# Spare times of an RWKV stage's small products, set place by place

## The chip, the cores and the metric

The kernel runs on one core of a Trainium2 chip. The metric is the time of one execution on the device in microseconds. Below, PE is the engine of the matrix products (TensorE), DVE is VectorE, ACT is ScalarE, POOL is GpSimd, and SP is the engine that issues most transfers (SyncE).

## The reference

One layer of a hybrid decoder is computed for 1024 prompt tokens and 8 x 8 sampled tokens, 1088 columns in all, in float32. Cut to what matters:

```python
h = rms_norm(x, norm_mix) * (1 + sc) + sh            # sc, sh, gt from c
P = h @ w_in                                          # 1024 -> 4352 columns
pr, pp, pg = split(P)                                 # RWKV, pooling, gates
# RWKV-7, 8 heads of 64:
def step(S, inp):
    sa = einsum("bhvk,bhk->bhv", S, -kk_t)
    S = S * w_t + sa * (kk_t * a_t) + v_t * k_t       # outer products
    return S, einsum("bhvk,bhk->bhv", S, r_t)
y = group_norm(y) + bonus;  o_r = y * (sigmoid(xg) @ g2)
o_p = causal means over windows 2, 4, 8, 16, minus the token, @ pool_w
merged = sig(g_r) * (o_r @ w_br_rwkv) + sig(g_p) * (o_p @ w_br_pool)
x = x + gt * (merged @ w_out)
x = x + gt2 * (square(relu(adaLN(x) @ w_ff1)) @ w_ff2)
y = rms_norm(x)
```

## The kernel before

All rows lie with features on the 128 partitions and tokens along the free axis. A float32 product with a weight is made of three products in a faster format, from a high and a low half of each operand (`whi`, `wlo` for weights; `hx` tiles for the rows). The 1088 columns are taken in three chunks of 364, 362 and 362, one PSUM bank each (`mm`, four banks). A job of such big products accumulates over eight blocks of weights for each chunk and is then emptied to SBUF by ACT (into `px`), or, in the eight last jobs of the stage (`op_job`), by DVE.

The first part of the kernel, up to about 702 us of the profile, is the stage in question. PE's stream of big products (`w_in`, the gates, then `op_job`) is the background, and the RWKV-7 recurrence runs beside it as a set of small products in the banks `w` (two) and `wc` (two). Four pairs of heads are worked one after the other, `f` = 0 to 3, and called head f below. The steps of each:

- `front(f)`: loads k and others from scratch in DRAM (`d_x`) into `wt` buffers (there are five), squares k on ACT, takes the norm of kk by `strips` (four small products, a square root on ACT, a reciprocal on DVE) and `fan` (a store to DRAM and two loads that spread it), and makes two tanh products (`wa` with `w2a2`).
- `scores` with `unit`: masked products of 64 tokens with each other.
- `inverse` on DVE and `level` on PE: the inverse of a triangular block, by products of 32x32 (`n16` with `xd`, `nd` with `zd`, `ao` with `x32`, `pt` with `z`).
- `affine`: the generators `first(u)` (z with `at`, emptied by ACT and DVE into `at` and `uv`) and `second(u)` (`ab` with `at`), for the two halves u of the tokens.
- `chain`: the recurrence over chunks of 64 tokens, S.
- `bonus(f)` and `post(f - 1)`: the bonus, the group norm (`sums`, or for the last head `piece` on each chunk), the output gate (`gate`), and a store of the result to `d_or`. For f = 3 post's rows stay in SBUF.

`pools` does the pooling branch's four products of three chunks each, tile `plw`.

The order of PE's instructions is written out by the program as it runs a planner: `Pace.run` keeps a time `t` that each product moves on by an estimated duration. It takes the next background product unless one of the generators (`chains`, `heads`, `pools`, `or_rows`) is due. A generator yields a `Need`: operands, banks, `wait`, `spare` and `slack`. It is due when

```python
def at(self):
    return max([self.k.clocks.ready(*self.aps) + self.spare] + [self.k.clocks.free(b, self.k.pb[b], self.banks.count(b)) + self.slack for b in set(self.banks)])
```

is at most `t`. Here `ready` is the planner's estimate of when the operands are there, and `spare` the nanoseconds that are added to it, 300 if nothing is given. So a larger spare puts a small product behind more big products in PE's order; it is not a wait on the chip. With `wait=0` a due product goes at once; otherwise it may be held back up to that many ns for a place where PE's mode changes anyway. When the background has nothing to give, `t` is moved on to the next due time, and the spare changes no order.

Once PE's order stands, `Ledger.schedule` plans the DVE instructions and the SP transfers against it with estimated durations, and `Ledger.fix` ties both engines to that order. ACT and POOL get theirs from the framework's own estimate of a time line. ACT and DVE take their instructions one after the other. A product of PE waits on the chip until its operands are there and its bank is empty.

Of the kernel before, what the change touches and what calls it, by code (L numbers as in the profile page):

```python
# [450 lines left out]
class Room:  # L451


    wait = 0
# [91 lines left out]
class K:  # L546
# [563 lines left out]
    def pools(self):  # L1110

        nc = self.nc
        self.pl = {}
        for g in range(4):
            plw = self.pxp.tile([P, P], F32, tag="plw", bufs=1, name=self.nm("plw"))
            nc.sync.dma_start(plw, self.io["pool_w"][:, g * 128:(g + 1) * 128])
            yield lambda: ("pool", g) in self.done
            z, zs, hi, lo = self.pl[g]
            for c0, n in CH:
                m = min(n, NPR - c0)  # L1120
                yield self.need(z[:, c0:c0 + m], plw, zs, wait=0, spare=6000)
                ps = self.ps("w")
                self.mm(ps[:, :m], plw, z[:, c0:c0 + m], start=True, stop=True)
                if m < n:
                    self.mm(ps[:, m:n], plw, zs, start=True, stop=True)
                sc = self.par("pool_scale", g)
                nc.scalar.activation(hi[:, c0:c0 + n], ps[:, :n], AF.Copy, scale=sc)
                nc.vector.scalar_tensor_tensor(lo[:, c0:c0 + n], ps[:, :n], sc, hi[:, c0:c0 + n].bitcast(F32), op0=ALU.mult, op1=ALU.subtract)
            nc.sync.dma_start(self.d_op[0][g], hi.bitcast(F32))
            nc.sync.dma_start(self.d_op[1][g], lo.bitcast(F32))  # L1130
            self.done.add(("op", g))


    def front(self, f):

        nc, io = self.nc, self.io
        fs = slice(f * 128, (f + 1) * 128)
        X = lambda b: lambda: ("X", b) in self.done
        w2a2 = self.sm.tile([P, P], F32, tag="sw", bufs=2, name=self.nm("sw"))
        nc.sync.dma_start(w2a2, io["w2a2"][:, fs])  # L1140
        yield X(12)
        wa = self.wt()
        nc.sync.dma_start(wa, self.d_x[12])
        yield X(4 + f)
        k, kk = self.wt(), self.wt()
        nc.sync.dma_start(k, self.d_x[4 + f])
        for c0, n in FH:
            nc.scalar.activation(kk[:, c0:c0 + n], k[:, c0:c0 + n], AF.Square, scale=self.par("k_k", f))
        yield self.need(kk, wait=0)
        self.strips(kk, 1.0, 1)  # L1150
        self.fan(kk, self.d_n[f])
        t1, tha = self.wt(), self.wt()
        for c0, n in FP:
            yield self.need(wa, w2a2, banks=("w", "w"))
            ps = self.ps("w")
            self.mm(ps[:, :n], w2a2[0:64, :], wa[0:64, c0:c0 + n], start=True, stop=True)
            nc.scalar.activation(t1[:, c0:c0 + n], ps[:, :n], AF.Tanh, bias=self.hp[:, f:f + 1], scale=0.5)
            ps = self.ps("w")
            self.mm(ps[:, :n], w2a2[64:128, :], wa[64:128, c0:c0 + n], start=True, stop=True)
            nc.scalar.activation(tha[:, c0:c0 + n], ps[:, :n], AF.Tanh, bias=self.hp[:, 4 + f:5 + f], scale=0.5)  # L1160
        yield self.need(kk, banks=(), wait=0)
        yield X(f)
        r = self.wt(wa)
        nc.sync.dma_start(r, self.d_x[f])
        e = self.row(self.p1, "e", 1, w=1112)
        ev = e[:, :1040].rearrange("p (c j) -> p c j", j=65)
        es = e[:, 1040:1112].rearrange("p (c j) -> p c j", j=9)
        nc.gpsimd.memset(ev[:, :, 0], 1.0)
        nc.gpsimd.memset(es[:, :, 0], 1.0)
        end = self.sm.tile([P, 24], F32, tag="end", bufs=2, name=self.nm("end"))  # L1170
        bk = self.p1.tile([P, NC, 2, 64], F32, tag="bk", bufs=1, name=self.nm("bk"))
        if f:
            yield lambda: ("c", f - 1, 0) in self.done
        for c0, n in FH:
            s, cs = slice(c0, c0 + n), slice(c0 // 64, (c0 + n) // 64)
            t, a, x = t1[:, s], tha[:, s], k[:, s]
            yield self.room()
            nc.vector.tensor_scalar(t, t, 1.0, None, op0=ALU.add)
            nc.vector.tensor_tensor_scan(t, self.kscan[:, :n], t, 0.0, ALU.mult, ALU.add)
            m = min(n, NPR - c0)  # L1180
            nc.scalar.activation(ev[:, c0 // 64:(c0 + m) // 64, 1:65], cut(t1[:, c0:c0 + m]), AF.Exp, scale=-HC)
            if m < n:
                nc.scalar.activation(es[:, :, 1:9], cut8(t1[:, NPR:NT]), AF.Exp, scale=-HC)
            nc.scalar.activation(t, t, AF.Exp, scale=HC)

            yield self.room()
            nc.vector.scalar_tensor_tensor(kk[:, s], x, self.par("k_k", f), kk[:, s], op0=ALU.mult, op1=ALU.mult)
            g = bk[:, cs, 0, :]
            nc.vector.tensor_scalar(g, cut(a), self.hp[:, 8 + f:9 + f], self.hp[:, 12 + f:13 + f], op0=ALU.mult, op1=ALU.add)
            yield self.room()  # L1190
            nc.vector.tensor_tensor(cut(x), cut(x), g, op=ALU.mult)
            nc.vector.scalar_tensor_tensor(a, a, 1.0, kk[:, s], op0=ALU.add, op1=ALU.mult)
            for h, hs in enumerate(HB):
                yield self.room()
                nc.vector.tensor_tensor(bk[hs, cs, h, :], cut(x[hs]), cut(t[hs]), op=ALU.mult)
                nc.vector.scalar_tensor_tensor(bk[hs, cs, 1 - h, :], cut(a[hs]), 0.5, cut(t[hs]), op0=ALU.mult, op1=ALU.mult)
            if c0 == 0:
                yield self.room()
                self.cur = dict(bk=bk, end=end, kk=kk, r=r, ev=ev, es=es, z=self.z, qs={})
                self.ra(self.cur, 0)  # L1200
        nc.gpsimd.tensor_copy(end[:, 0:16], ev[:, :, 64])
        nc.gpsimd.tensor_copy(end[:, 16:24], es[:, :, 8])
        yield X(8 + f)
        yield self.room()
        nc.vector.scalar_tensor_tensor(k, r, self.par("r_k", f), k, op0=ALU.mult, op1=ALU.mult)
        q = [self.wt(x, F32R) for x in (t1, tha)]
        self.halves(k, *q)
        v = self.wt(k)
        nc.sync.dma_start(v, self.d_x[8 + f])
        self.cur.update(q=q, v=v)  # L1210
# [163 lines left out]
    def level(self, d):  # L1374

        nc = self.nc
        ao, zd, xd, n16, z = d["ao"], d["zd"], d["xd"], d["n16"], self.z
# [7 lines left out]
                self.mm(at(ps, g, c), n16[g, c, :], xd[g, c, :], **tp(g))  # L1385
        nd = cut32(self.hv())
        nc.vector.tensor_tensor(nd, cut32(ps), self.kc("i32").unsqueeze(1).to_broadcast([P, 16, 32]), op=ALU.add)
        yield self.need(nd, zd)
        ps = self.ps("w")
        for c in range(16):  # L1390
            for g in G:
# [9 lines left out]
        for c in range(16):  # L1401
            for os in HB:
                lo = slice(os.start, os.start + 32)
# [17 lines left out]
    def affine(self, f, d):  # L1421


        nc, z = self.nc, d["z"]
# [40 lines left out]
        yield self.need(z, A[0], banks=("w", "w"))  # L1465
        beside(first(0))
        if f:
            yield self.need(z, *A, B[0], banks=("w", "w", "wc", "wc"))
            beside(first(1, 0.55), second(0, "wc", 0.55))
        else:  # L1470
            yield self.need(A[0], B[0], banks=("w", "w"))
            beside(second(0))
        self.done.add(("s", f, 0))
        if not f:
            yield self.need(z, A[1], banks=("w", "w"))
            beside(first(1))
        yield self.need(A[1], B[1], banks=("w", "w"))
        beside(second(1))
# [102 lines left out]
    def post(self, f):  # L1581
# [10 lines left out]
        def gate(*over):  # L1592
# [3 lines left out]
            nc.sync.dma_start(sg, self.d_x[13])  # L1596
            nc.sync.dma_start(bv, self.d_bv[f])
            for c0, n in CH:
                yield self.need(g2, sg[:, c0:c0 + n], wait=0)
                ps = self.ps("w")  # L1600
                self.mm(ps[:, :n], g2, sg[:, c0:c0 + n], start=True, stop=True)
                nc.scalar.activation(sg[:, c0:c0 + n], ps[:, :n], AF.Copy)
# [7 lines left out]

        def piece(c0, n):
            s = slice(c0, c0 + n)
            yield self.need(y[:, s], wait=0)
            ps = self.ps("w")
            self.mm(ps[:, :n], self.kc("bones"), y[:, s], start=True, stop=True)
            nc.vector.scalar_tensor_tensor(y[:, s], ps[:, :n], -1.0 / 64, y[:, s], op0=ALU.mult, op1=ALU.add)
            nc.scalar.activation(sq[:, s], y[:, s], AF.Square)
            yield self.need(sq[:, s], wait=0)
            ps = self.ps("w")
            self.mm(ps[:, :n], self.kc("bones"), sq[:, s], start=True, stop=True)  # L1620
            self.rinv(ps, n, sq[:, s], 1.0 / 64, 2)
# [17 lines left out]
        else:  # L1639
# [2 lines left out]
                self.halves(y[:, c0:c0 + n], hi[:, c0:c0 + n], lo[:, c0:c0 + n])  # L1642
            for c0, n in CH:
                s = slice(c0, c0 + n)
                yield self.need(hi[:, s], lo[:, s], wait=0)
                nc.vector.scalar_tensor_tensor(y[:, s], self.sums(hi[:, s], lo[:, s]), -1.0 / 64, y[:, s], op0=ALU.mult, op1=ALU.add)
                nc.scalar.activation(sq[:, s], y[:, s], AF.Square)
            yield self.need(sq, wait=0)
            self.strips(sq, 1.0 / 64, 2)
            self.fan(sq, self.d_n[4 + f])  # L1650
            yield self.need(sq, banks=(), wait=0)
            nc.vector.tensor_tensor(y, y, sq, op=ALU.mult)
            nc.scalar.activation(y, y, AF.Identity, bias=self.par("ln_b", f), scale=self.par("ln_w", f))
            yield self.need(y[:, 0:1], banks=(), wait=0)
            bv, sg = yield from gate(sq, hi)
            nc.vector.tensor_tensor(y, y, bv, op=ALU.add)
            nc.vector.tensor_tensor(y, y, sg, op=ALU.mult)
# [867 lines left out]
```

## Time and profile before

| what | value |
|---|---|
| median of 3 runs | 1579.59 us (1578.9 to 1580.49) |
| the profiled execution | 1579.88 us |
| its span, first to last instruction | 1577.5 us |
| stage of this change | about 54 to 702 us of the span |
| PE busy in the stage | 627.52 of 648.00 us |
| mean granted clock of PE, whole span | 0.991 |

Busy time is not time at full speed: the clock that the profile lists as granted to PE falls to one half in a few short stretches, and PE counts as busy in them. Of a wait the profile names the engine and the tile of the instruction that came last before it ended; "issue" means that it shows nothing that was waited for. Most engine instructions go through helpers, so that the line is L583 (products) or L402 (the rest), and the tiles tell them apart: `w<-wt,bones` and `w<-wt,kct` with 128x36x columns are group norm sums, `w<-wt,kct` with 128x272 are strips, `w<-ab,at` is `second`, `w<-at,z` is `first`, `w<-px,plw` is the pooling product.

### The profile page before, as it was taken

The numbers are of one execution on the slowest core, as the hardware profiler recorded it, in microseconds if no ns is written. First come the engines' busy times: TensorE is split into PE (matmuls) and PEld (weight loads), VectorE is DVE, ScalarE is ACT, GpSimd is POOL, SyncE is SP. The second block draws the span as 40 slices with busy tenths as digits, with TensorE's granted clock in tenths as the row PEclk, the third lists the DMA queues.
The fourth block names the chain that finished last, engine by engine and source line by source line (L and its number), as shares of the span: only waits on it lengthen the run. The fifth ranks groups of instructions, "written<-read, shape, count | busy, mean of one in ns | idle before, by whom it ended". The sixth has DMA issues, their size and how long they took to land.

```text
span 1577.5 us, 34072 instructions
## 1 busy us (share of the span) xinstructions
PE 1529.9 (97%) x13836; PEld 1428.5 (91%) x13836; DVE 1064.3 (67%) x1883; ACT 642.3 (41%) x1254; POOL 143.8 (9%) x231
## 2 busy tenths in 40 slices
PE   6999999999999998999999999999999999999997
PEld 2989788988998898889999999999999999999997
DVE  4476657948693856364545797899667796666776
ACT  5554353454335433331323572222334344334652
POOL 2100100000000000013501310000000050000000
PEclk9999999999999999999999999999999999999999
DMA  9242523345334424846874565665446996664754
GB/s 368 84 137 95 193 78 101 115 137 158 104 114 164 114 92 141 325 159 226 310 281 172 190 205 171 223 232 181 146 144 227 399 347 202 208 215 144 232 174 148
DMA packets 140412, 294.00 MB, mean 186 GB/s; under 512 B 37256, under 2 KB 44992, under 8 KB 140256
## 3 DMA queue, kind: packets, MB, share of 16 engines
q1 hardware_dynamic: 133872, 270.71, 50.2%
q10 hardware_dynamic: 4320, 14.00, 2.6%
q0 software_dynamic: 2064, 7.13, 1.4%
q8 instruction: 108, 1.77, 0.5%
q14 instruction: 48, 0.39, 0.1%
HBM read 214.44 MB, written 77.34 MB: 185 GB/s over the span
## 4 chain that ended last, share of the span: by engine, by line
PE 68%; DVE 6%; DMA 5%; ACT 2%; issue 1%; POOL 0%; SPq 0%; DVEq 0%; ACTq 0%; POOLq 0%
PE mm L583 46%; PE wc L583 11%; PE w L583 10%; DMA hid<-in_w_ff 2%; DVE hx L402 1%; DVE wlo L402 1%; DMA wt<-d_x 1%; DVE hv L402 1%; DMA t<-d_th 1%; DVE wt L402 1%; DMA hid<-in_w_ada_mlp 1%; DMA mg<-in_w_ff 1%; DVE mg L402 0%; ACT wt L402 0%; DMA wt<-d_n 0%
## 5 line engine op out<-in xcount | busy, mean ns | idle before, releaser
L583 PE MATMUL mm<-hx,whi 128*128 128x362 f32 (+2 forms) x2944 | 689.6, 322 | 8.5 <-ACT px L402 4.6
L583 PEld LDWEIGHTS mm<-hx,whi 128*128 128x128 f32 x2944 | 496.3, 189 | 31.6 <-issue 9.0
L583 PE MATMUL mm<-hx,wlo 128*128 128x362 f32 (+2 forms) x1472 | 462.5, 315 | 0.4 <-DVE wlo L402 0.4
L583 PEld LDWEIGHTS mm<-hx,wlo 128*128 128x128 f32 x1472 | 278.8, 190 | 1.4 <-issue 0.8
L583 PE MATMUL mm<-mg,whi 128*128 128x272 f32 (+2 forms) x1312 | 248.8, 288 | 2.2 <-ACT t L402 1.2
L583 PEld LDWEIGHTS mm<-mg,whi 128*128 128x128 f32 x1312 | 205.3, 188 | 7.2 <-issue 2.5
L583 PE MATMUL mm<-mg,wlo 128*128 128x272 f32 (+2 forms) x656 | 188.5, 287 | 0.0
L583 PE MATMUL wc<-hx,whi 128*128 128x272 f32 x896 | 170.4, 287 | 0.0
L402 ACT ACTIVATE whi<-hid 128x512 fp32r<-128x512 f32 x128 | 80.5, 630 | 150.5 <-PE mm L583 58.4
L583 PEld LDWEIGHTS wc<-hx,whi 128*128 128x128 f32 x896 | 140.3, 188 | 0.0
L583 PE MATMUL wc<-hx,wlo 128*128 128x272 f32 x448 | 128.8, 287 | 0.7 <-DVE wlo L402 0.7
L583 PEld LDWEIGHTS mm<-mg,wlo 128*128 128x128 f32 x656 | 123.5, 188 | 0.0
L402 DVE TENSOR_TENSOR wlo<-hid,whi 128x512 fp32r<-128x512 f32 x128 | 87.8, 688 | 44.6 <-ACT whi L402 43.5
L402 DVE TENSOR_TENSOR wlo<-wraw,whi 128x512 fp32r<-128x512 f32 x84 | 59.8, 713 | 64.9 <-ACT whi L402 63.4
L402 ACT ACTIVATE whi<-wraw 128x512 fp32r<-128x512 f32 x100 | 62.6, 628 | 99.0 <-PE mm L583 53.9
L583 PE MATMUL w<-hx,whi 128*128 128x272 f32 (+1 forms) x480 | 97.2, 296 | 0.0
L402 POOL TENSOR_TENSOR hx<-hx,rs 128x64 f32<-128x64 f32 x24 | 37.1, 1546 | 567.6 <-ACT hx L402 357.8
L583 PEld LDWEIGHTS wc<-hx,wlo 128*128 128x128 f32 x448 | 84.2, 188 | 0.9 <-DVE wlo L402 0.9
L583 PEld LDWEIGHTS w<-hx,whi 128*128 128x128 f32 x480 | 77.1, 188 | 0.8 <-issue 0.8
L583 PEld LDWEIGHTS mm<-mg,hx 128*128 128x128 f32 x576 | 72.8, 188 | 5.0 <-issue 5.0
L583 PE MATMUL mm<-mg,hx 128*128 128x272 f32 (+2 forms) x576 | 74.7, 289 | 0.0
L583 PE MATMUL w<-hx,wlo 128*128 128x272 f32 (+1 forms) x240 | 70.5, 295 | 0.2 <-DVE wlo L402 0.2
(292 smaller groups left out, 2209.5 us busy)
## 6 DMA issues: line engine op xcount, KB each, us to landing
t<-d_t SPq DMA_DIRECT2D x56, 544.0 KB, 4.5
hid<-in_w_ff SPq DMA_DIRECT2D x110, 256.0 KB, 4.0
d_t<-hx SPq DMA_DIRECT2D x102, 272.0 KB, 2.2
hid<-in_w_ff SPq DMA_DIRECT2D x42, 512.0 KB, 3.9
wraw<-in_w_in SPq DMA_DIRECT2D x68, 256.0 KB, 2.8
mg<-in_w_ff SPq DMA_DIRECT2D x58, 256.0 KB, 5.3
hid<-in_w_ada_mlp SPq DMA_DIRECT2D x24, 512.0 KB, 5.3
d_th<-px SPq DMA_DIRECT2D x22, 544.0 KB, 3.3
```

The costliest lines, as they stand in the source:

```text
L402: r = f(*a, **kw)
L583: r = self.nc.tensor.matmul(out, lhsT, rhs, **kw)
```

## The change

Only numbers of `spare` change: in `pools` 6000 becomes 6700; the places in `front`, `affine`, `gate`, `piece`, the sums, the strips and the row `y` of `post` go from the default 300 to 600, 1000 or 1500; the second need of `level` goes from 300 to 100. The estimated durations, the instructions and the transfers are the same.

```diff
 pools:   - yield self.need(z[:, c0:c0 + m], plw, zs, wait=0, spare=6000)
          + yield self.need(z[:, c0:c0 + m], plw, zs, wait=0, spare=6700)
 front:   - yield self.need(kk, wait=0)
          + yield self.need(kk, wait=0, spare=600)
          - yield self.need(wa, w2a2, banks=("w", "w"))
          + yield self.need(wa, w2a2, banks=("w", "w"), spare=600)
 level:   - yield self.need(nd, zd)
          + yield self.need(nd, zd, spare=100)
 affine, f > 0:
          - yield self.need(z, *A, B[0], banks=("w", "w", "wc", "wc"))
          + yield self.need(z, *A, B[0], banks=("w", "w", "wc", "wc"), spare=600)
 affine, f = 0:
          - yield self.need(A[0], B[0], banks=("w", "w"))
          + yield self.need(A[0], B[0], banks=("w", "w"), spare=600)
          - yield self.need(z, A[1], banks=("w", "w"))
          + yield self.need(z, A[1], banks=("w", "w"), spare=1500)
 post, gate:
          - yield self.need(g2, sg[:, c0:c0 + n], wait=0)
          + yield self.need(g2, sg[:, c0:c0 + n], wait=0, spare=600)
 post, piece (f = 3):
          - yield self.need(y[:, s], wait=0)
          + yield self.need(y[:, s], wait=0, spare=1000)
          - yield self.need(sq[:, s], wait=0)
          + yield self.need(sq[:, s], wait=0, spare=1000)
 post, f < 3:
          - yield self.need(hi[:, s], lo[:, s], wait=0)
          + yield self.need(hi[:, s], lo[:, s], wait=0, spare=1000)
          - yield self.need(sq, wait=0)
          + yield self.need(sq, wait=0, spare=600)
          - yield self.need(y[:, 0:1], banks=(), wait=0)
          + yield self.need(y[:, 0:1], banks=(), wait=0, spare=1000)
```

More of the change, by code (lines that the diff above doesn't have):

```diff
@@ L1120, in pools @@
                 m = min(n, NPR - c0)
-                yield self.need(z[:, c0:c0 + m], plw, zs, wait=0, spare=6000)
+                yield self.need(z[:, c0:c0 + m], plw, zs, wait=0, spare=6700)
                 ps = self.ps("w")
@@ L1148, in front @@
             nc.scalar.activation(kk[:, c0:c0 + n], k[:, c0:c0 + n], AF.Square, scale=self.par("k_k", f))
-        yield self.need(kk, wait=0)
+        yield self.need(kk, wait=0, spare=600)
         self.strips(kk, 1.0, 1)
@@ L1153, in front @@
         for c0, n in FP:
-            yield self.need(wa, w2a2, banks=("w", "w"))
+            yield self.need(wa, w2a2, banks=("w", "w"), spare=600)
             ps = self.ps("w")
@@ L1387, in level @@
         nc.vector.tensor_tensor(nd, cut32(ps), self.kc("i32").unsqueeze(1).to_broadcast([P, 16, 32]), op=ALU.add)
-        yield self.need(nd, zd)
+        yield self.need(nd, zd, spare=100)
         ps = self.ps("w")
@@ L1467, in affine @@
         if f:
-            yield self.need(z, *A, B[0], banks=("w", "w", "wc", "wc"))
+            yield self.need(z, *A, B[0], banks=("w", "w", "wc", "wc"), spare=600)
             beside(first(1, 0.55), second(0, "wc", 0.55))
         else:
-            yield self.need(A[0], B[0], banks=("w", "w"))
+            yield self.need(A[0], B[0], banks=("w", "w"), spare=600)
             beside(second(0))
@@ L1474, in affine @@
         if not f:
-            yield self.need(z, A[1], banks=("w", "w"))
+            yield self.need(z, A[1], banks=("w", "w"), spare=1500)
             beside(first(1))
@@ L1598, in gate @@
             for c0, n in CH:
-                yield self.need(g2, sg[:, c0:c0 + n], wait=0)
+                yield self.need(g2, sg[:, c0:c0 + n], wait=0, spare=600)
                 ps = self.ps("w")
@@ L1612, in piece @@
             s = slice(c0, c0 + n)
-            yield self.need(y[:, s], wait=0)
+            yield self.need(y[:, s], wait=0, spare=1000)
             ps = self.ps("w")
@@ L1617, in piece @@
             nc.scalar.activation(sq[:, s], y[:, s], AF.Square)
-            yield self.need(sq[:, s], wait=0)
+            yield self.need(sq[:, s], wait=0, spare=1000)
             ps = self.ps("w")
@@ L1644, in post @@
                 s = slice(c0, c0 + n)
-                yield self.need(hi[:, s], lo[:, s], wait=0)
+                yield self.need(hi[:, s], lo[:, s], wait=0, spare=1000)
                 nc.vector.scalar_tensor_tensor(y[:, s], self.sums(hi[:, s], lo[:, s]), -1.0 / 64, y[:, s], op0=ALU.mult, op1=ALU.add)
                 nc.scalar.activation(sq[:, s], y[:, s], AF.Square)
-            yield self.need(sq, wait=0)
+            yield self.need(sq, wait=0, spare=600)
             self.strips(sq, 1.0 / 64, 2)
@@ L1653, in post @@
             nc.scalar.activation(y, y, AF.Identity, bias=self.par("ln_b", f), scale=self.par("ln_w", f))
-            yield self.need(y[:, 0:1], banks=(), wait=0)
+            yield self.need(y[:, 0:1], banks=(), wait=0, spare=1000)
             bv, sg = yield from gate(sq, hi)
```

## The prediction

> **What bounds the kernel now.** First the page: the busy shares and the chain that ended last.
>
> ```profile
> span 1577.5 us, 34072 instructions
> PE 1529.9 (97%) x13836; PEld 1428.5 (91%) x13836; DVE 1064.3 (67%) x1883; ACT 642.3 (41%) x1254; POOL 143.8 (9%) x231
> PE 68%; DVE 6%; DMA 5%; ACT 2%; issue 1%; POOL 0%; SPq 0%; DVEq 0%; ACTq 0%; POOLq 0%
> ```
>
> TensorE (PE) is busy for 97% of the span and holds 68% of the chain, so an order of work can only win what PE loses to waits. Second, the table by stretches, cut where the RWKV stage begins and ends:
>
> ```profile
> core 0: us, PE busy (x) PEld busy (x) DVE busy (x) ACT busy (x) POOL busy (x), PEclk, DMA share, GB/s
> 54.00:702.00 648.00, 627.52 (x6881) 558.35 (x6880) 410.19 (x761) 278.71 (x590) 46.00 (x133) 0.99 0.43 138
> 702.00:1568.00 866.00, 861.72 (x6710) 847.24 (x6709) 620.43 (x1065) 332.20 (x619) 89.58 (x72) 1.00 0.63 218
> ```
>
> The stage that the change touches has 648.00 - 627.52 = 20.5 us of idle PE; the rest of the kernel behind it loses 4.3 us in 866. Third, whom PE waits for inside the stage (microseconds in total, times, longest):
>
> ```profile
> PE mm L583 <- ACT px L402: 4.6, 3, 2.0
> PE w L583 <- issue: 4.0, 5, 1.5
> PE wc L583 <- DVE S L402: 2.5, 2, 1.9
> PE w L583 <- ACT uv L402: 2.4, 2, 2.0
> PE mm L583 <- DVE px L402: 2.3, 1, 2.3
> PE w L583 <- DVE wt L402: 2.0, 2, 1.6
> ```
>
> These six groups have 17.8 us together, most of it. Only the waits of small products (tiles w and wc) stand at a place that a need sets; the mm rows are big products of the projection that wait until ACT or DVE has emptied a bank. Fourth, PE in order of time, to see which wait is which (start, duration, in brackets the idle time before it):
>
> ```profile
> 117.39 0.60 PE L583 MATMUL mm<-hx,whi 128*128 128x362 f32 x2 [2.01 <-ACT px L402]
> 260.77 0.37 PE L583 MATMUL wc<-S,ra 64*64 64x64 f32 x2 [1.91 <-DVE S L402]
> 354.75 1.09 PE L583 MATMUL w<-ab,at 64*64 64x128 f32 x16 [0.42 <-ACT uv L402]
> 459.10 0.57 PE L583 MATMUL w<-wt,bones 128*128 128x362 f32 x2 [1.56 <-DVE wt L402]
> 480.96 0.88 PE L583 MATMUL w<-px,plw 128*128 128x364 f32 x2 [1.49 <-issue]
> 511.50 3.05 PE L583 MATMUL w<-ab,at 64*64 64x128 f32 x32 [1.96 <-ACT uv L402]
> 611.04 0.65 PE L583 MATMUL w<-wt,kct 128*32 128x272 f32 x4 [1.27 <-ACT wt L402]
> 615.40 0.59 PE L583 MATMUL mm<-hx,whi 128*128 128x362 f32 x2 [1.53 <-ACT px L402]
> 699.88 0.60 PE L583 MATMUL mm<-hx,whi 128*128 128x362 f32 x2 [2.29 <-DVE px L402]
> ```
>
> Fifth, the granted clock behind the four waits near 2 us (the last columns are clock, DMA share and GB/s):
>
> ```profile
> 117.39:124.00 6.61, 6.61 (x48) 6.26 (x49) 6.60 (x13) 3.17 (x8) 1.75 (x6) 1.00 0.54 177
> 260.77:268.00 7.23, 7.23 (x58) 6.66 (x58) 2.87 (x6) 1.39 (x6) 0.00 (x0) 0.57 0.22 79
> 512.00:514.00 2.00, 1.95 (x26) 1.71 (x24) 1.46 (x4) 1.16 (x3) 0.00 (x0) 0.69 0.04 8
> 514.00:516.00 2.00, 2.00 (x34) 1.67 (x32) 0.16 (x1) 0.38 (x1) 0.00 (x0) 0.50 0.45 115
> 700.00:702.00 2.00, 2.00 (x7) 1.47 (x8) 1.60 (x4) 0.18 (x2) 0.00 (x0) 0.62 0.41 128
> 702.00:704.00 2.00, 2.00 (x8) 2.00 (x8) 1.48 (x2) 0.88 (x2) 0.00 (x0) 0.53 0.68 279
> ```
>
> PE counts as busy here and still loses time: (1 - 0.57) x 7.23 = 3.1 us behind the wait of 1.91, 0.6 + 1.0 = 1.6 behind that of 1.96, and 0.8 + 0.9 = 1.7 behind that of 2.29. So a wait near 2 us can cost nearly double or more. It need not: behind the 2.01 us at 117 (first row) the clock is 1.00. The pool is thus 20.5 + 6.4 = 26.9 us, or 1.7%, and the question is how much of it these needs reach.
>
> **The change part by part.** No instruction is added or removed. A larger spare lets big products, three at a time, go ahead of a small product; this costs no PE work. The orders of DVE and of SP's transfers are then planned anew from PE's, and ACT's follows. Each edit:
>
> *Pools, 6000 to 6700.* One wait stands here, the 1.49 us at 480.96, and the profile names nobody for it. Bounds: -0.7 if z was late, +0.7 for a gate job held for the pooled rows. I take 0. The other "issue" waits stand inside runs of 32x32 products, and this one directly behind such a run, so it is nearest to those, which no need sets.
>
> *kk's strips and the tanh products of front, 300 to 600; the gate products, 300 to 600.* None of the waits above is theirs: 0, with the big products as cover. Behind the strips go their store and two spreading loads on SP, 0.3 us later. The bounds are -0.3 and +0.3 per head.
>
> *nd, 300 to 100.* It brings the second block product 0.2 us forward; no data wait stands before it. Bounds: +0.2 in each of four heads, and -0.2 each for the chain behind. I take 0.
>
> *Sums in post, 300 to 1000.* The third chunk of head 1 waits 1.56 us at 459.10 for DVE to empty a bank. With 0.7 us more of big products ahead of it the wait is 0.9: -0.7, bounds 0 and -1.56.
>
> *Strips in post, 300 to 600.* The 1.27 us at 611.04 falls by 0.3. But the big products at 615.40 wait for ACT, which stands behind the same strips, and the 0.3 us of work put ahead is missing there. The wait moves on: 0, bounds -0.3 and +0.3.
>
> *affine, 300 to 600 (one place at head 0 to 1500).* Head 0 shows no such wait: 0. At heads 1 and 2 the product behind the changed one waits for uv, 0.42 and 1.96 us. At head 1, -0.3. At head 2 ACT's own order is the cause (SP's store, the load's piece from the chain of waits, then ACT):
>
> ```profile
> 499.91 0.61 SPq L402 DMA_DIRECT2D d_orh<-wt  x1
> 501.07 8.64 DMA wt<-d_x
> 509.80 1.39 ACT L402 ACTIVATE wt<-wt,part 128x512 f32<-128x512 f32 x2 [3.11 <-DMA wt<-d_x]
> 511.09 0.36 ACT L402 ACTIVATE uv<-w 64x256 f32<-64x256 f32 x1
> 354.32 0.38 ACT L402 ACTIVATE uv<-w 64x256 f32<-64x256 f32 x1 [1.87 <-DVE uv L402]
> 357.85 1.39 ACT L402 ACTIVATE wt<-wt,part 128x512 f32<-128x512 f32 x2 [3.15 <-DMA wt<-d_x]
> ```
>
> At head 2 the square of the next front's k, which waits for a load of 8.64 us, stands ahead of the uv eviction; at head 1 it stands behind. The load stands on SP behind the store of post's result, because it needs a buffer that post frees. So what delays post delays the load: 0.7 (sums), 0.3 (strips), 0.7 (y) and 0.3 (gate), 2.0 us at most, against 0.6 by which the affine products themselves move. Bounds: +2.0 - 0.6 = +1.4 and 1.6 more of half clock, so +3.0; and -1.96 - 1.6 = -3.6 if the order becomes that of head 1. I take 0, between the two: each delay can hide behind a transfer that is late anyway.
>
> *Pieces of post for head 3, twice 300 to 1000.* They end the stage:
>
> ```profile
> 690.63 0.77 PE L583 MATMUL w<-wt,kct 128*128 128x362 f32 x2
> 693.73 1.38 PE L583 MATMUL w<-wt,kct 128*128 128x362 f32 x4
> 695.44 0.49 PE L583 MATMUL mm<-hx,whi 128*128 128x364 f32 x2
> 695.13 2.43 DVE L402 RECIPROCAL wt<-wt 128x182 f32<-128x182 f32 x2 [3.16 <-ACT wt L402]
> 699.30 0.96 DVE L402 SCALAR_TENSOR_TENSOR px<-px,mm 128x364 f32<-128x364 f32 x2
> 709.80 0.54 DVE L402 TENSOR_TENSOR hx<-wt,hx 128x362 fp32r<-128x362 f32 x1
> 701.88 23.63 PE mm L583 x137
> ```
>
> The second mean (690.63) and its variance (693.73) lead to two reciprocals, 2.43 us, and only at 699.30 does DVE empty the banks of the running job of big products. Its first chunk (364 wide) ended at 695.44 + 0.49, near 696.0. That order makes the 2.29 us of PE. With 0.7 us more at each of the two products the reciprocals start 1.4 later, at 696.5. The first bank is then full before them, DVE can empty it by 696.6, and the whole wait of 2.3 goes if it takes a second bank between the reciprocals. If the second bank comes after both, at 696.6 + 2.4 + 0.5 = 699.5, PE, which wants it at about 698.1 (one chunk of 0.5 us after the 697.6 at which it stops now), waits 1.4, and only 0.9 is won. I take the middle, -1.6; the wait left, 0.7, is far under 2 us, and with it the half clock goes, -1.7. Bounds: 0 (the block stays together) and -4.0. That the tail ends later costs nothing by itself: post's last rows are written at 710.3, and PE runs on without a break until 725.5.
>
> **The sum:** -0.7 - 0.3 - 1.6 - 1.7 = -4.3 us. The profiled execution took 1579.88 (its span 1577.5 and 2.4 around it), so 1575.6; the median of the three runs is 1579.59, 0.3 lower, so I predict 1575.3. What a measurement of this kernel can tell from no change is 0.2%, 3.2 us: below 1576.4 is faster, above 1582.8 slower.
>
> The Trainium skill, "TensorE: Matmul & The Clock Gate", Why this matters for your kernels, says that only idle gaps above about 3 us bring the half clock back. By it, a shorter wait at 699.88 would return no clock, and the sum would be -2.6. The trace speaks against it here: three stretches at about half clock follow idle times of 1.91 to 2.29 us.
>
> **The rivals.** *Slower: ACT waits for the load at two heads.* Place: the uv evictions of heads 1 and 2. For it: head 2 has that order already. Against it: at head 1 the square came 3.5 us after the eviction. It decides as soon as head 1's square is put ahead: the load there lands by 357.8, so uv would be written at 359.1 and PE go on at about 359.2 instead of 354.75, +4.4, with 1.7 of half clock. With head 2 at its upper bound, +3.0, it is 9.1 on top of -4.3: 1584.4.
>
> *No change: the block at 697 stays together.* DVE's planned order puts post's older work first, and the eviction of the big products last, as now. Then -0.7 - 0.3 = -1.0 is left: 1578.6. For it: the planner prefers what was issued earlier, and the reciprocals are issued before the job ends.
>
> *The half clock stays.* The slow stretch at 700 comes from the thinner mix of products and not from the wait. Then 1.7 of the sum is lost: 1577.0. For it: the 2.01 us at 117 left the clock alone, so length by itself does not decide; against it: three of the four waits near 2 us have it. It is what the page named above would give too.
>
> *Faster by more:* head 2's square falls behind the evictions as at head 1, -3.6 more: 1571.7. It belongs to the faster side, as does a wait at 260.77 (1.91 and 3.1 us) that DVE's new order happens to dissolve.
>
> **How the numbers follow.** The forecast, with the case faster by more, 0.50; the block stays 0.18; the half clock stays 0.09; slower 0.23. So faster 0.50, same 0.27, slower 0.23. The forecast is no safer than that because its largest terms hang on how DVE and ACT are ordered anew, not on a wait that a need itself sets. The range that leaves out 2 in 10 goes from 1570.0, a little under the case faster by more, to 1583.5, into the slower case short of its full price. The likeliest case's own range is 1570.0 to 1576.4.
>
> **What would show it.** Right: at about 460 the bones product waits under 1 us; near 700 the mm product waits under 1 us for DVE and the clock stays at 1.00; the stage's idle PE falls from 20.5 to about 18. Wrong: a wait for uv over 3 us at heads 1 or 2, with the square of k ahead of it on ACT; a new mm wait of about 2 us for px elsewhere, with a stretch of half clock behind it; or post's last rows written after PE has run out of big products, which now leave 15 us.

## The result, and the profile after

| kernel | median, us | ratio to before, 95% interval |
|---|---|---|
| before | 1578.9 (7 runs, 1577.15 to 1580.89) | |
| after the change | 1568.96 (7 runs, 1563.66 to 1575.97) | 0.9936 (0.9913 to 0.9959) |
| after, run again beside e10 to e12 | 1566.26 (6 runs) | 0.9929 (0.9903 to 0.9956) |

The change is faster by 0.6 to 0.7%, about 10 us. The forecast was 1575.3, 4.3 us, with a range that began at 1570.0: the sign was right, the forecast gain was less than half of what came, and the measured median lies 1.0 us outside the range.

The profiled execution after took 1568.79 us, span 1566.4. To compare the two traces, the stage is taken to its very end here, up to the first big product in a bank w (its row, then the busy times and the clock from 54 us up to it):

```profile
726.49 0.49 PE L583 MATMUL w<-hx,whi 128*128 128x362 f32 x2
54.00:726.50 672.50, 652.02 (x7024) 582.85 (x7023) 422.14 (x782) 283.31 (x597) 48.59 (x137) 0.99 0.43 139
```

That is before; after, the same two rows read:

```profile
709.59 0.49 PE L583 MATMUL w<-hx,whi 128*128 128x362 f32 x2
54.00:709.60 655.60, 645.62 (x7022) 579.23 (x7021) 422.47 (x784) 282.68 (x598) 48.10 (x137) 0.99 0.44 143
```

The stage ends 16.9 us earlier. Idle PE (the length of the stretch less its busy time) falls from 20.5 to 10.0 us, which is 10.5 of it. Whom PE waits for now, in the window of the table shown before:

```profile
PE mm L583 <- ACT px L402: 2.6, 2, 2.2
PE w L583 <- issue: 2.1, 3, 1.0
PE w L583 <- ACT uv L402: 1.2, 3, 0.6
PE w L583 <- ACT iv L402: 1.0, 1, 1.0
PE wc L583 <- DVE S L402: 0.8, 1, 0.8
PE w L583 <- ACT wt L402: 0.7, 1, 0.7
PE w L583 <- DVE d L402: 0.5, 2, 0.4
PE w L583 <- DVE wt L402: 0.5, 1, 0.5
```

The 2.29 us for px on DVE are gone, the 1.96 for uv, the 1.91 for S at 260.77, the 1.56 for a bones bank and the 1.49 of "issue" at the pooling product too. Only one wait over 1.1 us is left, early in the stage. Three of those left, and two behind the stage (757 and 760):

```profile
117.24 0.60 PE L583 MATMUL mm<-hx,whi 128*128 128x362 f32 x2 [2.24 <-ACT px L402]
243.57 0.27 PE L583 MATMUL wc<-S,ra 64*64 64x64 f32 x2 [0.80 <-DVE S L402]
613.18 0.65 PE L583 MATMUL w<-wt,kct 128*32 128x272 f32 x4 [0.75 <-ACT wt L402]
757.05 1.05 PE L583 MATMUL wc<-hid,sT 128*32 128x512 f32 x4 [1.65 <-DMA hid<-in_w_ada_mlp]
759.68 1.92 PE L583 MATMUL wc<-hid,sT 128*32 128x512 f32 x4 [1.58 <-DMA hid<-in_w_ada_mlp]
117.24:121.00 3.76, 3.76 (x23) 3.13 (x23) 3.76 (x7) 2.46 (x5) 1.51 (x4) 0.58 0.41 115
243.57:250.00 6.43, 6.43 (x39) 4.29 (x40) 5.47 (x10) 1.47 (x4) 1.31 (x3) 0.73 0.23 36
759.70:763.50 3.80, 3.80 (x12) 2.14 (x13) 0.55 (x2) 0.00 (x0) 0.00 (x0) 0.57 1.05 404
```

The last three rows give the clock behind three of these waits. The time lost at half clock inside the stage is (1 - 0.58) x 3.76 + (1 - 0.73) x 6.43 = 3.3 us, where it was 6.4: 3.1 more of the 16.9. This part changes from one execution to the next, as the last section shows. The other 3.3 us lie in PE's busy time; what they are stays open.

Of the 16.9 us, 11.1 are left at the end of the span (1577.5 to 1566.4). PE now waits longer for the weights of the second modulation, the one of the MLP half (tile `hid`). Before, its only wait there was this one:

```profile
773.82 1.05 PE L583 MATMUL wc<-hid,sT 128*32 128x512 f32 x4 [0.54 <-DMA hid<-in_w_ada_mlp]
```

After, it waits 1.65 + 1.58 us, and loses (1 - 0.57) x 3.80 = 1.6 at half clock: 4.3 us more together. For the first of these products PE was ready 17.9 us earlier than before (755.4 against 773.3), and the load let it start 16.8 us earlier (757.05 against 773.82). So the loads came forward too, but not quite by as much as PE. The DMA share there is 1.05.

### The profile page after: what moved, and what is told of

Its sections match the earlier page's. It is cut to its first block, busy times and chain, and to the rows that moved or that the text cites. A ratio compares the mean times of both kernels' runs of the same rounds, so it can differ in the third digit from the quotient of the medians.

```text
span 1566.4 us, 34084 instructions
## 1 busy us (share of the span) xinstructions
PE 1525.2 (97%) x13836; PEld 1426.0 (91%) x13836; DVE 1064.2 (68%) x1883; ACT 642.1 (41%) x1254; POOL 142.4 (9%) x231
## 4 chain that ended last, share of the span: by engine, by line
PE 75%; DVE 8%; DMA 5%; ACT 2%; issue 2%; POOL 0%; SPq 0%; DVEq 0%; ACTq 0%; POOLq 0%
PE mm L583 50%; PE w L583 12%; PE wc L583 12%; DVE hx L402 2%; DMA hid<-in_w_ff 2%; DMA wt<-d_x 1%; DVE wlo L402 1%; DVE wt L402 1%; DMA hid<-in_w_ada_mlp 1%; DVE hv L402 1%; DMA t<-d_th 1%; PE w L621 1%; DVE bk L402 0%; DMA mg<-in_w_ff 0%; ACT wt L402 0%
## 5 line engine op out<-in xcount | busy, mean ns | idle before, releaser
L583 PEld LDWEIGHTS mm<-hx,whi 128*128 128x128 f32 x2944 | 495.4, 189 | 27.7 <-issue 11.1
```

Source lines behind the costliest of these rows:

```text
L583: r = self.nc.tensor.matmul(out, lhsT, rhs, **kw)
```

## The experiments

**First round: parts alone, and other sizes.** Theory A: once a product moves, all orders behind it come out anew, and which waits result is a matter of the whole order. Theory B: each longer spare takes its own length off the wait at its place.

*e1, post's edits for heads 0 to 2 alone* (sums 1000, strips 600, row y 1000):

```diff
- yield self.need(hi[:, s], lo[:, s], wait=0)
+ yield self.need(hi[:, s], lo[:, s], wait=0, spare=1000)
- yield self.need(sq, wait=0)
+ yield self.need(sq, wait=0, spare=600)
- yield self.need(y[:, 0:1], banks=(), wait=0)
+ yield self.need(y[:, 0:1], banks=(), wait=0, spare=1000)
```

> The kernel before with the three larger spares of post for heads 0 to 2 alone (sums 1000, strips 600, row y 1000); PE's order differs from 306 us on. Theory A (orders dealt anew: once one small product moves, the planner's clock, DVE's and SP's orders and ACT's order all come out otherwise behind it, and coincidences that made PE wait are dissolved or made): most of the gain behind 306 us is here, stage idle down by 5 us or more, 1569 to 1574 us. Theory B (each longer spare takes its own length off the wait at its own place): only the waits of 1.56 at 459 and 1.27 at 611 shrink, by 0.7 and 0.3: 1577 to 1578.5 us.

Measured: 1579.37, ratio 1.0011 (0.9990 to 1.0031). No gain is seen. A's 1569 to 1574 is missed; the median misses B's 1577 to 1578.5 too, but the interval does not exclude it. PE in order of time, the load in the chain of waits, and ACT:

```profile
512.81 1.79 PE L583 MATMUL w<-wt,kct 128*32 128x272 f32 x8 [5.03 <-ACT wt L402]
505.10 6.85 DMA wt<-d_x
512.03 1.39 ACT L402 ACTIVATE wt<-wt,part 128x512 f32<-128x512 f32 x2 [4.84 <-DMA wt<-d_x]
```

The wait at 459 is gone here as well, and so are all the others of the trace before from there to 627: between 440 and 640 us only waits of up to 0.3 us are left, but for a new one of 5.03 us before the strips of kk of head 3. The load of k lands at 511.95, and PE's order has the strips ahead of that. So what the waits gave was in large part paid back by the order that followed. (In this profiled execution, one of the faster of the ten, the stage ends 6.9 us earlier than before and the span 3.1; the median shows nothing of it.)

*e2, level's and affine's edits alone* (nd 100; affine 600, 600 and 1500).

> The kernel before with the edits of level (300 to 100) and affine (600, 600, 1500) alone. Theory A: the order changes from 183 us on; the waits at 189 (1.07) and 221 to 261 (0.58 and 1.91, with 3.1 us of half clock) can go, the later ones are dealt anew: 2 to 6 us either way, 1573 to 1581. Theory B: no wait stands at these places but 0.42 at 354 and 1.96 at 511, one product behind them, less 0.3 each: 1578 to 1579.5 us.

Measured: 1577.58, ratio 0.9999 (0.9980 to 1.0017). This lies in A's range and within the noise of B's, so it does not tell them apart. The wait of 1.91 at 260.77 is gone in this trace, with one of 1.48 for another tile at 260.47 in its place; the later ones are as they were:

```profile
509.79 1.47 PE L583 MATMUL w<-ab,at 64*64 64x128 f32 x18 [2.32 <-ACT uv L402]
698.07 0.60 PE L583 MATMUL mm<-hx,whi 128*128 128x362 f32 x2 [2.29 <-DVE px L402]
```

*e3 and e4, all edits at half and at one and a quarter of their size*, for example the sums:

```diff
- yield self.need(hi[:, s], lo[:, s], wait=0, spare=1000)
+ yield self.need(hi[:, s], lo[:, s], wait=0, spare=650)     # e3
+ yield self.need(hi[:, s], lo[:, s], wait=0, spare=1180)    # e4
```

> All edits at half their size (sums 650, strips 450, level's 200, pools 6350 and so on). Theory A: another deal: anywhere between 1564 and 1582, with waits at other places than after the change. Theory B: about half of the gain of 10 us: 1573 to 1575 us.

> All edits at one and a quarter of their size (sums 1180, strips 680, affine 680 and 1800, pools 6880, level's 50). Theory A: again another deal, 1564 to 1582, waits at new places. Theory B: more slack at each place, so as fast as after the change or a little faster: 1566 to 1570 us.

Measured: e3 1586.35, ratio 1.0049 (1.0031 to 1.0067); e4 1584.2, ratio 1.0043 (1.0024 to 1.0061). Both are slower than before, and both lie beyond the 1582 that A had given as its bound. Theory B cannot have this: half of the slack and more of it both lose what the whole wins. In e3 (the first three rows) and e4 (the last) there are long waits at places of their own:

```profile
514.85 0.27 PE L583 MATMUL wc<-S,ra 64*64 64x64 f32 x2 [3.21 <-DVE S L402]
671.84 0.85 PE L583 MATMUL w<-wt,sw 128*128 128x364 f32 x2 [2.83 <-DMA wt<-d_x]
659.39 12.31 DMA wt<-d_x
676.14 1.46 PE L583 MATMUL w<-wt,sw 128*128 128x364 f32 x4 [2.86 <-DMA wt<-d_x]
```

The gate products of head 3 (`w<-wt,sw` with 128*128) stand in PE's order ahead of the landing of their rows, a load that takes 12.31 us in e3. (e3's trace is that of the slowest of its nine executions, 1593.01.)

**Second round: one edit left out.** Theory C, new: one edit makes nearly all of the gain.

*e5, e6, e7: the change without level's edit, without front's two, without post's three.*

```diff
- yield self.need(nd, zd, spare=100)                                  # e5
+ yield self.need(nd, zd)
- yield self.need(kk, wait=0, spare=600)                              # e6, and wa with w2a2
+ yield self.need(kk, wait=0)
- yield self.need(hi[:, s], lo[:, s], wait=0, spare=1000)             # e7, and sq, y
+ yield self.need(hi[:, s], lo[:, s], wait=0)
```

> The change with level's need left at 300. PE's order differs from 183 us on and falls back into that of the change (663 lines differ). Theory A (orders dealt anew; a good combination, its gain spread over the places where its order differs): only the part up to about 330 us is lost, the waits near 189 and 261 come back, 2 to 5 us slower than the change, 1571 to 1575. Theory C (one edit makes nearly all of the gain, and the rest is without effect): either no loss at all, 1568 to 1570, or all of it, 1578.

> The change with the strips of kk and the tanh products of front left at 300. None of the waits before stood at these places, but 3870 lines of PE's order differ from the change. Theory A: most of the gain goes although the edits have no wait of their own: 1572 to 1585. Theory C: no loss, 1568 to 1570, if front is not the one edit. Theory B (own place only) also 1568 to 1570.

> The change without the edits of post for heads 0 to 2 (pieces of head 3 keep theirs). Theory A: PE's order differs from 306 us on, so the gain behind it is lost or dealt anew: 1573 to 1582. Theory B: 1 us slower than the change, 1570. Theory C: 1578 if post is the one edit, but alone on the kernel before it gave nothing.

Measured: e5 1576.75, ratio 0.9986 (0.9966 to 1.0006); e6 1580.02, ratio 1.0003 (0.9985 to 1.0021); e7 1580.45, ratio 1.0007 (0.9988 to 1.0027). Leaving out any of the three loses nearly all or all of the gain, so C falls, and A holds but for the size in e5. Without post the waits near 460, 482, 514, 613, 617 and 625 are back, 1.3 to 2.3 us each. Front is the clearest: it has no wait of its own in the trace before, and without it PE waits at 512 as in e1. With it the strips come at 519.09, well behind the landing of their load at 510.89, and wait for nothing (e6, then the change):

```profile
511.86 1.80 PE L583 MATMUL w<-wt,kct 128*32 128x272 f32 x8 [4.59 <-ACT wt L402]
519.09 0.67 PE L583 MATMUL w<-wt,kct 128*32 128x272 f32 x8
```

So the two belong together: post's edits clear the waits from 459 to 627, and front's edits clear the one that post's order brings.

e5 lost more than its own stretch. PE, then POOL, then the landing in the chain of waits, then the clock:

```profile
666.56 0.48 PE L583 MATMUL w<-x,z 64*64 64x64 f32 x4 [6.80 <-POOL x L402]
665.62 0.54 POOL L402 DMA_DIRECT2D px<-d_th  x1 [18.62 <-DMA d_th<-px]
666.18 0.33 POOL L402 TENSOR_TENSOR x<-x,x 128x64 f32<-128x64 f32 x1
656.05 9.01 DMA d_th<-px
666.50:673.30 6.80, 6.74 (x69) 5.97 (x71) 3.10 (x6) 1.84 (x5) 0.01 (x1) 0.50 0.26 87
```

POOL issues the loads of `d_th` for `op_job`. One of them waits until a store out of the same px buffer has landed, at 665.06, and the small add of the sample's x stands behind it on POOL. After the change the add stands ahead of that load:

```profile
655.07 0.31 POOL L402 TENSOR_TENSOR x<-x,x 128x64 f32<-128x64 f32 x1 [8.81 <-DVE x L402]
659.87 0.56 POOL L402 DMA_DIRECT2D px<-d_th  x1 [4.49 <-DMA d_th<-px]
```

*e8, the change with later products of the second modulation* (the planner's time for its first products, in ns):

```diff
- (8500 if g else 16000, 8500, 8500, 8500), 3000)
+ (8500 if g else 20500, 8500, 8500, 8500), 3000)
```

> The change, and in the second part the first products with the weights of the second modulation 4.5 us later on the planner's clock (16000 becomes 20500). After the change PE waits 1.65 and 1.58 us there for these weights and loses 1.7 us at half clock, where before it waited 0.54. If the stage's gain of 17 us was given back here because the loads keep their own pace while PE came earlier, these 4.9 us return: 1564 to 1565 us. If the loads simply come later with the products, the wait stays and the time too, 1568 to 1570; a later modulation may also hold up the norm behind it, 1570 to 1575.

Measured: 1569.28, ratio 0.9947 (0.9927 to 0.9966). In its profiled execution the two waits for `hid` are gone, and two shorter ones stand there instead:

```profile
763.46 0.39 PE L583 MATMUL mm<-mg,whi 128*128 128x272 f32 x1 [0.57 <-ACT mg L402]
764.65 0.39 PE L583 MATMUL mm<-mg,whi 128*128 128x272 f32 x1 [0.79 <-DVE mg L402]
```

But the median stays at that of the change and does not show the 4 to 5 us that were expected of this. The profiled execution is the fastest of the eight, 1561.36: its stage had no half clock at all and ended 3.3 us earlier than after the change, with which e8's edit has nothing to do. So this one trace does not show what e8 is worth, and why the median gains nothing stays open.

**Third round: two single waits taken away.**

*e9, the change again, as a base for its neighbours.*

> The changed kernel itself, beside the next three on the same chip, so that they can be compared run by run: 1566 to 1571 us as before. Theories A and C agree.

Measured: 1566.26, ratio 0.9929 (0.9903 to 0.9956).

*e10, e5 with the loads on SP; e11, the change with them there:*

```diff
- nc.gpsimd.dma_start(th[:, :NT], self.d_th[8 + m])
+ nc.sync.dma_start(th[:, :NT], self.d_th[8 + m])
```

> The change without level's edit, which lost all of the gain, and the loads of d_th for op_job issued on SP and no longer on POOL. PE's and DVE's orders stay those of the kernel without level's edit. Theory A1 (what that kernel lost is one inversion on POOL: the add of the sample's x stands behind a load that waits for a store of the same buffer to land, and PE waited 6.8 us for x with as much again at half clock): the wait at 667 goes and 1567 to 1571 are reached. Theory A2 (the loss is many small waits in the orders of PE and DVE): no difference, 1575 to 1578.

> The change with those loads on SP. In the change the add stands ahead of the load, so A1 expects no gain, 1567 to 1571, or up to 2 us in runs in which a load on POOL held something else; a loss of 1 to 4 us if SP's own queue is then held up by a store's landing ahead of loads of weights.

Measured: e10 1569.75, ratio 0.9941 (0.9921 to 0.9962); e11 1570.64, ratio 0.9949 (0.9929 to 0.9969). In e10 the add is done early, and its product follows without a wait:

```profile
658.61 0.32 POOL L402 TENSOR_TENSOR x<-x,x 128x64 f32<-128x64 f32 x1 [19.24 <-DVE x L402]
660.44 0.28 PE L583 MATMUL w<-x,z 64*64 64x64 f32 x4
```

A1 is right: with the loads on SP the kernel without level's edit (e10) is as fast as the one with it (e11), 0.9941 and 0.9949, and PE's order in e10 is that of e5, product for product. So nearly all that level's edit seemed to be worth was this one inversion on POOL, an engine that level's products do not use. The change itself gains nothing from the move: e11's 0.9949 beside e9's 0.9929 may even be the small loss that was thought possible, but the intervals overlap.

*e12, post's edits alone, and a long spare for the strips that waited:*

```diff
- yield self.need(kk, wait=0)
+ yield self.need(kk, wait=0, spare=5300 if f == 3 else 300)
```

> The kernel before with post's edits alone, which gave nothing, and 5300 in place of 300 for the strips of kk at head 3 alone. With post's edits alone PE waited 5.03 us there, because the planner took the load of k as landed long before it was. Theory B holds at this one place, since the wait is far longer than the spare was: it goes, with 1.7 us of half clock, and the time falls by 4 to 7 us to 1572 to 1575. Theory A without B: the wait is dealt to another place and the time stays at 1577 to 1581.

Measured: 1578.07, ratio 0.9994 (0.9977 to 1.0011).

```profile
512.58 1.32 PE L583 MATMUL w<-wt,kct 128*32 128x272 f32 x8 [0.99 <-ACT wt L402]
518.11 0.60 PE L583 MATMUL mm<-hx,whi 128*128 128x362 f32 x2 [1.14 <-ACT px L402]
```

The wait falls from 5.03 to 0.99, as B has it for a wait that is long beside the spare. The profile shows new ones behind it (1.14 here, 1.66 for S at 533), and the median does not come down to the 1572 to 1575 that B gave: a good part was dealt on, as A has it. How much is not shown, since the intervals of e1 and e12 overlap.

**Fourth round: the prediction's largest term, and the order without the size.**

*e13, the pieces' edit alone on the kernel before; e14, the change without it:*

```diff
- yield self.need(y[:, s], wait=0)          # e13; e14 the other way round
+ yield self.need(y[:, s], wait=0, spare=1000)
- yield self.need(sq[:, s], wait=0)
+ yield self.need(sq[:, s], wait=0, spare=1000)
```

> The kernel before with the two needs of post's pieces for head 3 at 1000 and nothing else. The prediction's largest term by itself: the 2.29 us of PE near 700 shrink to 0.7 or less and the half clock behind goes: -3.3 us, 1575 to 1576. If that term was right only by the chance that the tail falls elsewhere in a job of big products (theory A), the wait stays near 2 us: 1578 to 1580.

> The change with the pieces left at 300. If the pieces' edit is what takes the 2.29 us near 700 away, the wait is back: 3 to 4 us slower than the change, 1569 to 1573. Theory A: the tail begins elsewhere in a job than before anyway, so the wait need not come back: 1566 to 1570, within 1.5 us of the change.

Measured: e13 1575.83, ratio 0.9981 (0.9966 to 0.9996); e14 1570.19, ratio 0.9938 (0.9918 to 0.9959). In e13 the wait near 700 is gone, and the 0.57 us at 684.95 are all that PE waits for DVE's px (PE's row, then DVE's); in e14 a wait of the same kind is there, for a bank that DVE empties behind post's work (the last row):

```profile
684.95 0.60 PE L583 MATMUL mm<-hx,whi 128*128 128x362 f32 x2 [0.57 <-DVE px L402]
695.99 2.43 DVE L402 RECIPROCAL wt<-wt 128x182 f32<-128x182 f32 x2 [2.66 <-ACT wt L402]
699.16 0.97 DVE L402 SCALAR_TENSOR_TENSOR px<-px,mm 128x364 f32<-128x364 f32 x2
700.89 0.60 PE L583 MATMUL mm<-hx,whi 128*128 128x362 f32 x2 [1.80 <-DVE d L402]
```

e13's time is what the prediction's term gave, though its interval reaches from 0.6 to 5.4 us of gain. With the other edits in place the term is not shown: e14 is 1.7 us slower than e15 below, from the same round, by the ratios, and the intervals overlap.

*e15, all edits at three quarters of their size* (sums 820, strips 520, pools 6520 and so on).

> All edits at three quarters of their size. The planner's steps are coarse, and PE's order comes out as after the change but for two products of the tail that stand one group of big products earlier; SP and POOL have the same order. Theory A (the order alone counts): 1566 to 1570 as after the change, where half the size gave 1586. Theory B (slack counts by its size): a quarter of the gain lost, 1569 to 1572.

Measured: 1567.45, ratio 0.9927 (0.9902 to 0.9951). With a quarter less slack the whole gain is there. The interval alone does not exclude B's 1569 to 1572. But the orders of DVE, ACT, POOL and SP in this program are those of the change, and PE's differs in a few places at the end of the stage. Half of the slack, with another order, gave 0.5% more than before (e3). So the spare acts through the order that comes out, in coarse steps, and not through its nanoseconds.

No kernel of these is shown to be faster than the change.

## Why the prediction was wrong

*What bounds the kernel.* Right in the main: 13.6 of the 16.9 us are waits of PE in this stage and half clock, about half of the 26.9 that the prediction named as the pool. The other 3.3, in PE's busy time, are not in that pool.

*Pieces, -1.6 and -1.7.* The size agrees with e13, 0.9981 or -3.0 us for this edit alone, but that was luck, for the way was another. DVE still empties px behind the reciprocals (699.16 behind 695.99 in e13), but PE no longer stops: the job of big products and the reciprocals have moved against each other. What was foreseen, a bank emptied ahead of or between the reciprocals, did not happen. Nor does the trace of e13 show the half clock won: it is gone at 700, but stretches near 118, 262, 334 and 484 make 6.8 us in the stage, where there had been 6.4.

*Sums, -0.7.* The wait of 1.56 went altogether, in e1 too; but e1 as a whole gained nothing.

*affine, -0.3 at head 1.* Wrong. With the other edits in place, the programs with and without affine's three edits are identical, so these edits do nothing. The wait there is 0.65 us after the change, where it was 0.42. The rival on the slower side (ACT's square ahead of the evictions at head 1) did not come true either.

*The terms taken as 0: this is the step that failed.* Front, gate and level were given 0 because no wait stood at their places; pools, post's strips and the wait at head 2 were given 0 between bounds of either sign. But without front (e6), without level (e5) and without post (e7) nearly all or all of the gain is lost. The waits at 481, 511, 615 and 627, with 1.49 + 1.96 + 1.53 + 0.91 = 5.9 us, went altogether. The edits at 481 and 511 could take at most 0.7 and 0.3 of them by their length, and no edit stands at 615 and 627. The row of the last, before:

```profile
626.91 1.20 PE L583 MATMUL w<-hv,ao 32*32 32x32 f32 x64 [0.91 <-DVE hv L402]
```

What the runs showed in place of these zeros: post's three edits, priced at -0.7, dissolve the waits from 459 to 627 by the order that they bring (gone in e1; back in e7, but for the last); front's edits avoid the 4.6 to 5.0 us that this order costs at 512 (e1, e6); and level's edit keeps an add on POOL ahead of a load, where the other order costs 6.80 us and half clock (e5). For level's own products the 0 was right, as e10 beside e11 shows. The prediction said that the orders of DVE, SP and ACT would be dealt anew, and then summed as if they stayed, and POOL is in none of its terms. Its bounds came from moving one wait at a time, so the range ended at 1570.0.

*The sum also lacked what was given back:* 4.3 us at the second modulation, behind the stage, where the prediction let the idle time stay as it was. PE came forward by a little more than the loads behind the stage did.

*The rivals.* "The block stays together" resembles what e14 shows when the pieces' edit is missing. "The half clock stays" did not come about at 700. "Faster by more" came in size and not in its way: the wait of 1.96 at head 2 and its half clock went, but in the change k's square (510.96) still stands ahead of two uv evictions of head 2 (513.12 and 514.25), and PE has other products until then. The order that was foreseen, the square behind the evictions, is that of e1 and e6, and there PE waits 5.03 and 4.59 us for the strips. The wait at 260.77, the other part of that rival, went too; a wait of 0.80 at 243.57 with 1.7 us at half clock and one of 1.01 at 260.36 stand near it now. "Slower" did not come about for the change. Its neighbours e3 and e4, with the same edits in another size, are 0.4 to 0.5% slower, but not by the mechanism of that rival: their long waits are for S and for late loads, not for uv. So the risk was real, and its reason was another.

## What to carry to other kernels

When a planner turns margins into an order, a margin is not worth its length: ask what the order may become, not only what each wait loses, and let the range be as wide as the pool of waits allows. Here the pool was 1.7%; the change won 0.6 to 0.7, and neighbours of it lost 0.5. A setting like this one is good as a whole: taking one edit out of it, or scaling it, is a new setting and has to be measured. Look on every in-order engine, idle ones too, for a small instruction behind a transfer that waits: one such place on POOL cost 0.45% (0.9986 in e5, 0.9941 in e10), most of what all the edits together had won.

## What the runs showed of the hardware

An engine that is busy for only 9% of the span can stop PE for 6.8 us: in e5 a DMA issue on POOL that waits for another transfer's landing stands ahead of an add of 0.33 us.

The half clock is not tied to the length of the wait. The same product near 117 us shows it. After the change 2.24 us of waiting were followed by a clock of 0.58 over 3.76 us. In e15, whose program is the same up to there, the same wait left it at 1.00:

```profile
117.20 0.60 PE L583 MATMUL mm<-hx,whi 128*128 128x362 f32 x2 [2.24 <-ACT px L402]
117.20:121.00 3.80, 3.79 (x31) 3.44 (x32) 3.80 (x7) 2.46 (x5) 1.50 (x4) 1.00 0.39 125
```

The 2.01 us of before left it at 1.00 too, and so did 2.88 us in e5, while 1.55 us in e13 were followed by 0.68 over 3.84 us. At 243.57 a wait of 0.80 us after the change was followed by a stretch of 0.73 over 6.43 us, which is 3.5 us at one half. So what one trace loses at half clock is no fixed part of an order: over the stage it was 3.3 us after the change, and 1.7 in the trace of e9, the same kernel. Of the 13 executions of the changed kernel the two fastest (1562.23 and 1563.66) had a mean granted clock of 0.996, the two slowest (1575.75 and 1575.97) 0.991. A term of the sum that is half clock behind one wait, as the -1.7 at 700, is therefore a chance and not a price.

The Trainium skill, "TensorE: Matmul & The Clock Gate", Part 1, has the monitor watch free-running windows of about 3.4 us; the traces agree with the length of such a stretch (the 3.5 us above) and with its coming and going between runs. The same page, in Why this matters for your kernels, advises against idle gaps of more than about 3 us between bursts; here gaps of 0.80 to 2.3 us were followed by half clock too.
